# Loading cached keys by groups of 32 tokens instead of by head, in a hybrid decoder layer on one Trainium2 core

## The chip, the core and the metric

The kernel runs on one core of a Trainium2 chip. The core has five engines, each with an instruction queue of its own that is worked off in order: TensorE (PE; its weight loads are listed apart as PEld), VectorE (DVE), ScalarE (ACT), GpSimd (POOL) and SyncE (SP), which here issues transfers. A transfer is carried out by the core's 16 DMA engines, in packets. The metric is the device time of one execution in microseconds; less is better.

## The reference

One layer of a decoder serves a prompt of 512 tokens and a group of 8 sample sequences with 4 new tokens each, with the same weights, all in float32. Its three sub-layers are a mixer (4 mLSTM heads and 4 differential-attention heads), a cross-attention with 4 heads of 256 into 256 memory tokens, and a gated feed-forward network with a short causal convolution. What the change touches are the keys that the sample group reads from its caches:

```python
past_k = cache_dk[l][page_table].reshape(Bs, past_len, DA_HEADS, 2, DA_QK_DIM)   # 8 x 256 x 4 x 128

def mem_attend(h, mk, mv, w_mq, w_mo):
    q = (h @ w_mq).reshape(B, T, MEM_HEADS, MEM_HEAD_DIM)
    s = jnp.einsum('bqhd,bkhd->bhqk', q, mk) * (MEM_HEAD_DIM ** -0.5)            # mk: 8 x 256 x 4 x 256
    p = jax.nn.softmax(s, axis=-1)
    o = jnp.einsum('bhqk,bkhd->bqhd', p, mv).reshape(B, T, D_MODEL)
    return o @ w_mo
```

Per sequence there are two pages of 128 past tokens, found through `page_table`, with 4 heads of 128 (512 KB), and 256 memory tokens with 4 heads of 256 (1 MB). A cache row is one token: its heads lie side by side in DRAM.

## The kernel before

The kernel is one program for the Tile framework: it is written in a sensible order, and the framework's scheduler orders each engine's instructions and puts in the waits. Weights stream from DRAM through six staging tiles (`stage()`, named `wst`, 128 partitions x 1024), are split into a high and a low part by ScalarE (line 146) and VectorE (line 147) and then used by TensorE; transfers wait until such a tile is free. Large products are `gemmA` (lines 411 to 413) and `gemmB` (lines 472 and 485). All large loads go through SyncE's queue.

**Token keys** (`dk_load`, lines 1215 to 1221). For each of the 8 sequences a staging tile takes the keys of two pages. TensorE wants the key dimension on the partitions. So head h's 32 tokens out of a group are put on partitions 32h to 32h + 31, four groups of 32 tokens side by side, and `dk_turn` (line 1224) transposes 32 x 32 blocks in place on VectorE. Each transfer serves one head of one page: 32 partitions, on each of them 4 rows of 512 B from tokens that lie 32 apart; 8 transfers a sequence, 64 in all, 64 KB each. The page's number is read from a table, so a register operation stands ahead of each transfer. The scores (`dk_scores`, line 1251) go to `sc`, are summed into `pS` (line 1264) and are followed by the softmax. The prompt's differential attention (`da_soft`, `da_turn`, `da_av`: lines 1275 to 1305) is interleaved with this, a step at a time, and shares VectorE with it. Four of the six staging tiles hold mLSTM states until these are written out (line 1010), so six of the eight sequences are loaded after that, and then the values (line 1090, tile `vt`) and `w_out`.

**Memory keys** (`mk_load`, lines 1507 to 1513). For each sequence two tiles of 128 tokens, from the staging tiles (`wst`), the weight slots (`kvt`) or a spare tile. The layout is the same: 32 partitions for each head, 4 rows of 1,024 B on each, one transfer for each head of each half: 8 transfers a sequence, 64 in all, 128 KB each. `mk_turn` (line 1517) transposes each tile, 16 times in all. `gemmB`'s second half for the queries (line 485 with `hqT`; its results are taken from PSUM by lines 1439 and 1440, on ScalarE and VectorE) runs while the first sequences load. Then come the prompt's cross-attention (`ch_soft`, `ch_turn`, `ch_out`: lines 1460 to 1493), the sample group's scores (line 1529), their sum (line 1540) and softmax, the values (`mv_load`, line 1557, 512 KB each) and their product (line 1567, into `pso`). `oS` (line 1611) takes that from PSUM, `ost` (line 1614) transposes it, and the product with `w_mo` follows. The sample group's convolution state is loaded in the same stretch (lines 1626 to 1628).

The convolution outputs (lines 1785 and 1786, tile `cvr`) are transfers of another kind, which the prediction uses: they write 8 partitions to 2 x 4 rows of 512 B in DRAM, and 64 partitions to 16 x 4 rows.

Of the kernel before, what the change touches and what calls it, by code (L numbers as in the profile page):

```python
# [15 lines left out]
P = 128  # L16
# [4 lines left out]
NS = NB * TS  # L21
ROWS = SEQ + NS
H = 4
# [54 lines left out]
def kernel(ctx: ExitStack, tc: tile.TileContext, I, O):  # L78
# [29 lines left out]
    def T2(shape, name, dt=F32):  # L108
        return t2p.tile(list(shape), dt, name=name, tag="T2")
# [17 lines left out]
    def v2(t, b):  # L127
        return t.rearrange("p (a b) -> p a b", b=b)
# [10 lines left out]
    dma = nc.sync.dma_start  # L139
# [69 lines left out]
    def stage():  # L209
        return stg.tile([P, 1024], F32, name="wst", tag="st")  # L210
# [319 lines left out]
    for b in range(2):  # L530
        kept.append(norm_turn(xms[b], P, "g_mem_src", memT, b * P))
        if b == 0:

            t = turned[0].ins
            fill = mmp("fill")
            for _ in range(NFILL):
                with burst(t):
                    t = mm(fill, lhsT=warm[:, 0:P], rhs=warm, start=True, stop=True).ins
# [132 lines left out]
    for c0, c1 in HALF:  # L671
        n = c1 - c0
# [4 lines left out]
        t = T2([64, n], "gt")  # L677
# [253 lines left out]
    for g in range(2):  # L931
        for h in range(0, H, 2):
            t = stage().rearrange("p (j b e) -> p j b e", j=2, b=4)
# [38 lines left out]
    t = None  # L972
    for h in range(H):
        with burst(t):
            t = mm(pg[NS * h:NS * h + NS, P:2 * P + 1], lhsT=sm_t[:, h, :], rhs=vNs[:, h, :], start=True, stop=True).ins
    for h in range(H):
        with burst(t):
            t = mm(pg[NS * h:NS * h + NS, 4:12], lhsT=qT[:, h, SEQ:], rhs=nT[:, h, :], start=True, stop=True).ins
    for b in range(NB):
        for h in range(H):  # L980
            with burst(t):
                t = mm(pi[NS * h:NS * h + NS, 0:P], lhsT=qzm[:, 256 * h + b * NS:256 * h + (b + 1) * NS],
                       rhs=csts[b // 4, h][:, b % 4, :], start=(b == 0), stop=(b == NB - 1)).ins
# [101 lines left out]
    def page(name, b, g):  # L1085
        v = nc.sync.value_load(ptab[0:1, 2 * b + g:2 * b + g + 1], min_val=0, max_val=I[name].shape[1] - 1)
        return I[name][0, bass.ds(v, 1)]
# [120 lines left out]
    for b in range(4):  # L1208
        c = slice(b * P, b * P + P)
# [3 lines left out]
    kst, pts, aTs, outs, rcs = {}, {}, {}, {}, {}  # L1213

    def dk_load(b):
        st = kst[b] = stage()
        for g in range(2):
            src = page("cache_dk", b, g)
            for h in range(H):
                dma(out=v2(st[NS * h:NS * h + NS, 512 * g:512 * g + 512], P),  # L1220
                    in_=src[:, :, h].rearrange("n (k t) d -> t (n k) d", t=NS))

    def dk_turn(b):
        nc.vector.transpose(out=kst[b], in_=kst[b])
# [93 lines left out]
    for t, _ in enumerate(pipe(NB, dk_load, dk_turn, dk_scores)):  # L1318
        if t == 3:
            F.add(out_gate())  # L1320
        F.run(2.5)
        next(prompt)
        F.run(2.5)
# [86 lines left out]
    for q in range(2):  # L1410
        st = v2(stage(), 256)
        dma(out=st, in_=mk_d[:, 4 * q:4 * q + 4])
        split(mkT[0][:, 4 * q:4 * q + 4], mkT[1][:, 4 * q:4 * q + 4], st)
    for c in range(2):
        st = stage()
# [79 lines left out]
    kst, vts = {}, {}  # L1495
# [4 lines left out]
    def two(i):  # L1500

        if i < 3:
            return [stage(), stage()]
        t = wp.tile([P, 2, DM], F32, name="kvt", tag="W") if i < 7 else S([P, 2, DM], F32, "kvt")
        return [t[:, 0], t[:, 1]]

    def mk_load(b):

        kst[b] = two(home[b])
        for c in range(2):  # L1510
            for h in range(H):
                dma(out=v2(kst[b][c][NS * h:NS * h + NS], 256),
                    in_=I["cache_mem_k"][0, b, c * P:(c + 1) * P, h].rearrange("(k t) d -> t k d", t=NS))

    def mk_turn(b):
        for t in kst[b]:
# [2 lines left out]
    def mk_scores(bs):  # L1519

        t = None
        for b in bs:
            ps = mmp("ssc")[:, :256]
            for c in range(2):
                kv = kst[b][c].rearrange("p (k j t) -> p k j t", j=8, t=NS)
                for j in range(8):
                    g = NS * (j % 4)
                    with burst(t):
                        t = mm(v2(ps[g:g + NS, c * P:c * P + P], NS), lhsT=qx[:, j, b // 2 * 2:b // 2 * 2 + 2].rearrange("p n r -> p (n r)"),
                               rhs=kv[:, :, j, :], start=(j < 4), stop=(j >= 4)).ins  # L1530
            nc.scalar.copy(out=sc[:, b], in_=ps)
        return t
# [40 lines left out]
    for k in range(4):  # L1573
        mk_load(SEQS[k])
    for i, _ in enumerate(gemmB(hqT, [ev_q(m) for m in range(4, 8)])):
        if i % 4 == 1:
            mk_turn(SEQS[i // 4])
        if i % 4 == 3:
            mk_load(SEQS[4 + i // 4])
# [11 lines left out]
    t = mk_scores(SEQS[4:])  # L1591
# [205 lines left out]
    for gi, js in enumerate(groups):  # L1797
# [8 lines left out]
        def one(b, ps, i, s, cs=slice(0, 512)):  # L1806
            t = act[i // 2][:, i % 2]
            st, en = i == 0, i == nk - 1
            if b == 4:
                return sample_mm(ps, [acs[i], acs[i + 1]], s[1], i == 0, i == nk - 2)  # L1810
            s = s[0]
            c0 = b * P
            mm(ps, lhsT=t[:, 0, c0:c0 + P], rhs=s[:, 0, i % 2, cs], start=st, stop=False)  # L1813
            mm(ps, lhsT=t[:, 0, c0:c0 + P], rhs=s[:, 1, i % 2, cs], start=False, stop=False)  # L1814
            return mm(ps, lhsT=t[:, 1, c0:c0 + P], rhs=s[:, 0, i % 2, cs], start=False, stop=en)  # L1815
# [29 lines left out]
        if not last:  # L1845
            behind = []
            for n0 in (0, 512):
# [4 lines left out]
                for i in range(nk):  # L1852
# [3 lines left out]
                    for b in range(4):  # L1856
                        t = one(b, ps[b], i, s)
# [14 lines left out]
        def chunk(b, n0):  # L1872
            while len(wd) < (nk // 2 if n0 == 0 else nk):
                wd.append(W.get())
            w = 256 if (b, n0) == (TORD[-1], 512) else 512
            for o in range(0, 512, w):
                ps = mmp()[:, :w]
                for i in range(0, nk, 2 if b == 4 else 1):
                    t = one(b, ps, i, wd[(n0 and nk // 2) + i // 2], slice(o, o + w))
                add_y(b, ps, n0 + o, w)  # L1880
            return t
# [39 lines left out]
        t = chunk(TORD[1], 0)  # L1921

        for n0 in (0, 512):
            with burst(t.ins):
                t = chunk(TORD[0], n0)
# [78 lines left out]
```

## Time and profile before

| | before |
|---|---|
| median of 3 runs | 962.47 us (960.28 to 964.78) |
| profiled execution | 962.62 us, its span 960.9 us |
| granted TensorE clock, mean | 0.983 of full speed |
| TensorE busy, matmul / weight load | 918.8 us (96%) / 798.7 us (83%) |
| VectorE / ScalarE / GpSimd busy | 602.7 / 373.1 / 206.7 us |
| read from DRAM / written | 112.31 MB / 16.93 MB |
| token keys issued | 213.8 to 273.5 us after the span's start |
| memory keys issued | 401.6 to 447.8 us |

The span runs from the first to the last instruction. An engine's busy share is a mean over stages with different limits; what a stage is limited by is read from its waits. In a list of waits a row names who waited, for whom, and then the total, the number and the longest, in microseconds. In an engine's order of time a row has start, duration, engine, line, operation, out<-in and a count of merged instructions, and in brackets the idle time before it and what ended it. `SPq` rows are SyncE's transfers: the duration is that of the issuing instruction, not of the data. A DMA view of a window has the packets in it, their sizes and the share of the 16 engines' time that they took.

### The profile page before, as it was taken

To read this page: it belongs to the slowest core of one execution; us is meant where nothing else is said; L and a number is where in the kernel's file an instruction comes from. 1 tells how busy PE (TensorE), PEld (TensorE's weight loads), DVE (VectorE), ACT (ScalarE), POOL (GpSimd) and SP (SyncE) were. 2 spreads that over 40 slices of the span, in tenths; PEclk is the share of its full clock that TensorE was granted. 3 is DMA by queue.
4 is the path that set the end of the run, shared out by engine and by line. 5 is a ranking of instruction groups with operands and counts; after the bars stand their busy time and mean duration, and the time that the engine had idled before them with its cause. 6 is when DMAs were issued, how large, how long until landed. Compare 5 with 4: busy or idle time off the path is not lost. (4 is left out here: it accounts for less than half of the span.)

```text
span 960.9 us, 17244 instructions
## 1 busy us (share of the span) xinstructions
PE 918.8 (96%) x6584; PEld 798.7 (83%) x6584; DVE 602.7 (63%) x1108; ACT 373.1 (39%) x715; POOL 206.7 (22%) x422
## 2 busy tenths in 40 slices
PE   8999999999679999979979999999999999999995
PEld 5899787889546778979857899989988997999974
DVE  5846145654787338666644678727758676676767
ACT  5745233344366447613523534232212222122222
POOL 6610000107422216301000363101101110110114
PEclk9999999999899999989979999999999999999998
DMA  8950023353573339988752842053052412612023
GB/s 283 313 173 2 8 81 135 88 166 92 165 244 125 132 115 305 291 179 225 292 203 88 231 154 89 4 161 103 4 141 71 131 26 68 174 48 88 23 92 115
DMA packets 134498, 130.37 MB, mean 136 GB/s; under 512 B 10103, under 2 KB 104152, under 8 KB 134416
## 3 DMA queue, kind: packets, MB, share of 16 engines
q1 hardware_dynamic: 128232, 125.70, 43.2%
q10 hardware_dynamic: 6184, 3.57, 1.2%
q8 instruction: 52, 0.85, 0.4%
q14 instruction: 30, 0.25, 0.1%
HBM read 112.31 MB, written 16.93 MB: 135 GB/s over the span
## 5 line engine op out<-in xcount | busy, mean ns | idle before, releaser
L485 PE MATMUL mm<-fT,wslot 128*128 128x256 f32 x1872 | 236.0, 288 | 0.0
L485 PEld LDWEIGHTS mm<-fT,wslot 128*128 128x128 f32 x1872 | 234.4, 188 | 1.8 <-issue 0.8
L146 ACT CAST wslot<-wst 128x1024 fp32r<-128x1024 f32 x125 | 130.7, 1049 | 261.3 <-issue 80.4
L147 DVE TENSOR_TENSOR wslot<-wst,wslot 128x1024 fp32r<-128x1024 f32 x125 | 154.4, 1239 | 86.4 <-ACT wslot L146 85.9
L1814 PE MATMUL mm<-wslot,act 128*128 128x512 f32 (+1 forms) x180 | 70.2, 391 | 0.0
L1815 PE MATMUL mm<-wslot,act 128*128 128x512 f32 (+1 forms) x180 | 70.0, 392 | 0.0
L1813 PE MATMUL mm<-wslot,act 128*128 128x512 f32 (+1 forms) x180 | 69.3, 387 | 0.0
L1719 POOL COPY cvo<-u 128x2 f32<-128x2 f32 x43 | 10.4, 242 | 204.5 <-DVE u L1717 194.5
L411 PE MATMUL mm<-wslot,hT 128*128 128x512 f32 x128 | 51.3, 402 | 0.0
L413 PE MATMUL mm<-wslot,hT 128*128 128x512 f32 x128 | 51.0, 400 | 0.0
L412 PE MATMUL mm<-wslot,hT 128*128 128x512 f32 x128 | 50.8, 397 | 0.0
L485 PE MATMUL mm<-hT,wslot 128*128 128x256 f32 (+1 forms) x384 | 50.8, 289 | 0.0
L1714 DVE TENSOR_TENSOR u<-mm,rsb 128x256 f32<-128x256 f32 x43 | 18.1, 424 | 50.6 <-PE mm L485 50.3
L485 PEld LDWEIGHTS mm<-hT,wslot 128*128 128x128 f32 x384 | 49.1, 188 | 0.5 <-issue 0.2
L1813 PEld LDWEIGHTS mm<-wslot,act 128*128 128x128 f32 x180 | 34.3, 191 | 8.0 <-issue 0.8
L1815 PEld LDWEIGHTS mm<-wslot,act 128*128 128x128 f32 x180 | 33.8, 188 | 7.2 <-issue 0.4
L1814 PEld LDWEIGHTS mm<-wslot,act 128*128 128x128 f32 x180 | 33.8, 188 | 7.2
L1731 ACT ACTIVATE c<-c 128x560 f32<-128x560 f32 x21 | 14.1, 672 | 56.6 <-DVE c L1725 56.6
L1725 DVE SCALAR_TENSOR_TENSOR c<-u,cvT,c 128x560 f32<-128x560 f32 x43 | 34.3, 797 | 0.9
L1724 DVE SCALAR_TENSOR_TENSOR c<-u,cvT,c 128x560 f32<-128x560 f32 x43 | 34.1, 793 | 0.2
L485 PE MATMUL mm<-hqT,wslot 128*128 128x256 f32 x192 | 27.0, 305 | 5.0 <-ACT qs L1442 5.0
L485 PEld LDWEIGHTS mm<-hqT,wslot 128*128 128x128 f32 x192 | 26.4, 204 | 5.4 <-ACT qs L1442 5.4
(482 smaller groups left out, 1818.2 us busy)
## 6 DMA issues: line engine op xcount, KB each, us to landing
wst<-in_w_up_dram SPq DMA_DIRECT2D x42, 512.0 KB
wst<-in_w_in_dram SPq DMA_DIRECT2D x28, 512.0 KB
wst<-in_w_down_dram SPq DMA_DIRECT2D x20, 512.0 KB
kvt<-in_cache_mem_k_dram SPq DMA_DIRECT2D x40, 128.0 KB
kvt<-in_cache_mem_v_dram SPq DMA_DIRECT2D x10, 512.0 KB
wst<-in_w_mk_dram SPq DMA_DIRECT2D x8, 512.0 KB
xb<-in_x_prompt_dram SPq DMA_DIRECT2D x8, 512.0 KB
wst<-in_cache_dk_dram SPq DMA_DIRECT2D x64, 64.0 KB
```

Source lines behind the costliest of these rows:

```text
L146: nc.scalar.copy(out=hi, in_=src)
L147: (eng or nc.vector).tensor_tensor(out=lo, in0=src, in1=f32(hi), op=SUB)
L411: mm(ps[b], lhsT=xt.hi(k, c0, c0 + n), rhs=s[:, 0, kk, :], start=(k == 0), stop=False)
L412: mm(ps[b], lhsT=xt.hi(k, c0, c0 + n), rhs=s[:, 1, kk, :], start=False, stop=False)
L413: return mm(ps[b], lhsT=xt.lo(k, c0, c0 + n), rhs=s[:, 0, kk, :], start=False, stop=(k == nk - 1))
L485: mm(ps[i], lhsT=s[:, l, k, :], rhs=x(k, c0, c1), start=(k == 0 and j == 0), stop=(k == 7 and j == 2))
L1714: VTT(out=u[:, 2:258], in0=ps, in1=rsb[:, 0:256], op=MUL)
L1724: STT(out=c, in0=u[:, 1:EXT - 1], scalar=w[1], in1=c, op0=MUL, op1=ADD)
L1725: STT(out=c, in0=u[:, 0:EXT - 2], scalar=w[0], in1=c, op0=MUL, op1=ADD)
L1813: mm(ps, lhsT=t[:, 0, c0:c0 + P], rhs=s[:, 0, i % 2, cs], start=st, stop=False)
L1814: mm(ps, lhsT=t[:, 0, c0:c0 + P], rhs=s[:, 1, i % 2, cs], start=False, stop=False)
L1815: return mm(ps, lhsT=t[:, 1, c0:c0 + P], rhs=s[:, 0, i % 2, cs], start=False, stop=en)
```

## The change

The 8 transfers of a sequence's keys are cut in another way. Before, one transfer took one head and all four groups of 32 tokens. Now one takes one group of 32 tokens and all four heads. It writes 128 partitions with one row each, instead of 32 partitions with four rows each. In DRAM it reads 4 heads of 32 tokens, instead of 32 tokens of 4 groups. Each byte lands where it landed before; the number of transfers, their sizes and the rows' lengths (512 and 1,024 B) are the same, and so are the transposes and all that follows.

```diff
         for g in range(2):
             src = page("cache_dk", b, g)
-            for h in range(H):
-                dma(out=v2(st[NS * h:NS * h + NS, 512 * g:512 * g + 512], P),
-                    in_=src[:, :, h].rearrange("n (k t) d -> t (n k) d", t=NS))
+            for k in range(4):
+                dma(out=st[:, 512 * g + P * k:512 * g + P * k + P], in_=src[:, NS * k:NS * k + NS].rearrange("n t h d -> (n h) t d"))
...
         kst[b] = two(home[b])
         for c in range(2):
-            for h in range(H):
-                dma(out=v2(kst[b][c][NS * h:NS * h + NS], 256),
-                    in_=I["cache_mem_k"][0, b, c * P:(c + 1) * P, h].rearrange("(k t) d -> t k d", t=NS))
+            for k in range(4):
+                dma(out=kst[b][c][:, 256 * k:256 * k + 256], in_=I["cache_mem_k"][0, b, c * P + NS * k:c * P + NS * k + NS].rearrange("t h d -> h t d"))
```

The file is two lines shorter, so line numbers behind each place are one and two lower in the changed kernel. The scheduler makes a slightly different order of it. SyncE's queue at the memory keys, from the first of them to the first values (`wst` and `kvt` are the keys' and values' tiles, `cr` the convolution state), before:

```order
L1512 DMA kvt<-in_cache_mem_k_dram 32x4x256 x3
L1512 DMA wst<-in_cache_mem_k_dram 32x4x256 x8
L1512 DMA kvt<-in_cache_mem_k_dram 32x4x256 x5
L1512 DMA wst<-in_cache_mem_k_dram 32x4x256 x16
L1512 DMA kvt<-in_cache_mem_k_dram 32x4x256 x16
L1626 DMA cr<-in_state_conv_dram 16x896
L1512 DMA kvt<-in_cache_mem_k_dram 32x4x256 x8
L1627 DMA cr<-in_w_dw_dram 3x896
L1628 DMA cr<-in_b_dw_dram 1x896
L1626 DMA cr<-in_state_conv_dram 16x896
L1512 DMA kvt<-in_cache_mem_k_dram 32x4x256 x8
L1557 DMA wst<-in_cache_mem_v_dram 128x1024 x2
```

and with the change:

```order
L1511 DMA kvt<-in_cache_mem_k_dram 128x1x256 x2
L1511 DMA wst<-in_cache_mem_k_dram 128x1x256 x8
L1511 DMA kvt<-in_cache_mem_k_dram 128x1x256 x4
L1511 DMA wst<-in_cache_mem_k_dram 128x1x256 x4
L1511 DMA kvt<-in_cache_mem_k_dram 128x1x256 x2
L1511 DMA wst<-in_cache_mem_k_dram 128x1x256 x12
L1511 DMA kvt<-in_cache_mem_k_dram 128x1x256 x16
L1624 DMA cr<-in_state_conv_dram 16x896
L1511 DMA kvt<-in_cache_mem_k_dram 128x1x256 x16
L1555 DMA wst<-in_cache_mem_v_dram 128x1024 x6
```

The keys stand together as before, with the written shape 128 x 1 x 256 instead of 32 x 4 x 256; three small convolution loads have moved behind the keys, and the third tile's loads stand between two other tiles' loads.

VectorE's order at the third token sequence's transpose (the STREAM_TRANSPOSE; `mltm` belongs to the mLSTM's output gate, `rc` and `pda` to the prompt's softmax, `nm` is its maximum), before:

```order
L1045 TENSOR_TENSOR mltm<-mlt,soT 128x512
L1281 RECIPROCAL rc<-su 128x2
L1224 STREAM_TRANSPOSE wst<-wst 128x1024
L1045 TENSOR_TENSOR mltm<-mlt,soT 128x512
L1283 SCALAR_TENSOR_TENSOR pda<-pda,rc 128x128
L1045 TENSOR_TENSOR mltm<-mlt,soT 128x512
L1282 TENSOR_SCALAR rc<-rc,su,nlam 128x1
L1045 TENSOR_TENSOR mltm<-mlt,soT 128x128
```

and with the change:

```order
L1045 TENSOR_TENSOR mltm<-mlt,soT 128x512 x2
L1281 TENSOR_SCALAR rc<-rc,su,nlam 128x1 x2
L1045 TENSOR_TENSOR mltm<-mlt,soT 128x512
L1045 TENSOR_TENSOR mltm<-mlt,soT 128x128
L1282 SCALAR_TENSOR_TENSOR pda<-pda,rc 128x128
L1223 STREAM_TRANSPOSE wst<-wst 128x1024
L1282 SCALAR_TENSOR_TENSOR pda<-pda,rc 128x128
```

The gate's products and one `pda` step of the prompt have moved ahead of this transpose.

ScalarE's order where the sample group's cross-attention is taken from PSUM (`wslot<-wst` are casts of `w_mo`), as a piece of the difference:

```order
-L146 CAST wslot<-wst 128x1024 x3
-L1611 COPY oS<-pso 128x256
-L146 CAST wslot<-wst 128x1024
...
+L146 CAST wslot<-wst 128x1024 x2
+L1609 COPY oS<-pso 128x256
+L146 CAST wslot<-wst 128x1024
```

`oS` has moved ahead of the third cast of `w_mo`.

## The prediction

> **What bounds the kernel now.** I read the page first, then the list of waits on TensorE, then VectorE's and SyncE's instructions in order of time at the two places that the change touches, last the DMA views of short windows. The page and the waits:
>
> ```profile
> PE 918.8 (96%) x6584; PEld 798.7 (83%) x6584; DVE 602.7 (63%) x1108; ACT 373.1 (39%) x715; POOL 206.7 (22%) x422
> PE   8999999999679999979979999999999999999995
> ...
> PE ost L1614 <- ACT oS L1611: 6.1, 1, 6.1
> PE tpa L1291 <- DVE pda L1283: 5.2, 2, 5.0
> PE mm L485 <- ACT qs L1442: 5.0, 2, 3.8
> ```
>
> TensorE is the bound, 96% busy, and has few holes; but the three longest lie at the token keys (the 6 and the 7 of the second row, 240 to 288 us, in slices of 24 us) and at and behind the memory keys (the next two 7s, from 408 and from 480 us). Behind the second and the third stands VectorE, which transposes each key tile when it has landed and takes everything else behind it in order:
>
> ```profile
> 254.22 1.25 DVE L1224 STREAM_TRANSPOSE wst<-wst 128x1024 f32<-128x1024 f32 x1 [3.08 <-DMA wst<-in_cache_dk_dram]
> 258.73 1.25 DVE L1224 STREAM_TRANSPOSE wst<-wst 128x1024 f32<-128x1024 f32 x1 [0.20 <-DMA wst<-in_cache_dk_dram]
> ...
> 275.93 1.23 DVE L1224 STREAM_TRANSPOSE wst<-wst 128x1024 f32<-128x1024 f32 x1
> ...
> 413.24 1.25 DVE L1517 STREAM_TRANSPOSE wst<-wst 128x1024 f32<-128x1024 f32 x1 [7.40 <-DMA wst<-in_cache_mem_k_dram]
> ...
> 433.08 1.25 DVE L1517 STREAM_TRANSPOSE kvt<-kvt 128x1024 f32<-128x1024 f32 x1 [1.23 <-DMA kvt<-in_cache_mem_k_dram]
> 435.40 1.25 DVE L1517 STREAM_TRANSPOSE kvt<-kvt 128x1024 f32<-128x1024 f32 x1 [1.08 <-DMA kvt<-in_cache_mem_k_dram]
> ...
> 452.02 1.23 DVE L1517 STREAM_TRANSPOSE kvt<-kvt 128x1024 f32<-128x1024 f32 x1
> ```
>
> The bracket is VectorE's idle time and what ended it. Both key streams already set its pace: a token sequence (8 transfers) every (275.93 - 254.22) / 5 = 4.34 us, half a memory sequence (4 transfers) every 2.3 to 2.4 us. So there is almost no slack ahead of either stream. What paces them is seen on SyncE and in the DMA views (427 to 436 us for the memory keys, 256 to 266 for the token keys, 285 to 289 for w_out):
>
> ```profile
> 213.77 0.43 SPq L1220 DMA_DIRECT2D wst<-in_cache_dk_dram  x1
> ...
> 224.95 0.32 SPq L1220 DMA_DIRECT2D wst<-in_cache_dk_dram  x1
> ...
> 253.67 20.19 SPq L1220 DMA_DIRECT2D wst<-in_cache_dk_dram  x38
> ...
> 401.62 3.65 SPq L1512 DMA_DIRECT2D kvt<-in_cache_mem_k_dram  x3
> ...
> 427.26 8.97 SPq L1512 DMA_DIRECT2D kvt<-in_cache_mem_k_dram  x16
> ```
>
> ```profile
> DMA packets 2190, 2.00 MB, mean 222 GB/s; under 512 B 241, under 2 KB 2190, under 8 KB 2190
> ```
>
> ```profile
> DMA packets 2748, 1.28 MB, mean 128 GB/s; under 512 B 303, under 2 KB 2746, under 8 KB 2746
> q1 hardware_dynamic: 2746, 1.25, 45.2%
> wst<-in_cache_dk_dram SPq DMA_DIRECT2D x19, 64.0 KB
> ```
>
> ```profile
> DMA packets 814, 1.51 MB, mean 378 GB/s; under 512 B 76, under 2 KB 76, under 8 KB 814
> ```
>
> Token keys: 20.19 / 38 = 0.53 us a transfer with the DMA engines 45% busy, so SyncE's issuing paces them. Memory keys: about 0.6 us a transfer at 222 GB/s, where w_out reaches 378 GB/s with all 128 partitions, so the transfer itself paces them. The smallest packets close a transfer, one for each DMA engine that took part: 19 token transfers and 303 of them, 16 each.
>
> **The change, part by part.** The bytes and the 64 + 64 transfers stay. Each now writes 128 rows of one head-and-token block, but reads DRAM as 4 heads by 32 tokens; before, both sides had 32 rows. The trace has a pair of that kind, the convolution outputs: L1785 writes 8 partitions to 2 x 4 rows (4 KB), L1786 64 partitions to 16 x 4 rows (32 KB). Their issue, beside today's keys (min/median/max ns), and their packets, in a window that holds the packets of the 4 KB one alone and in one with both:
>
> ```profile
> L1220 SPq DMA_DIRECT2D wst<-in_cache_dk_dram x64: 316/317/1236, 213.8 to 273.5; - x64
> L1512 SPq DMA_DIRECT2D kvt<-in_cache_mem_k_dram x40: 311/430/2693, 401.6 to 447.8; - x40
> L1785 SPq DMA_DIRECT2D out_dram<-cvr x10: 644/657/772, 605.6 to 917.6; - x10
> L1786 SPq DMA_DIRECT2D out_dram<-cvr x10: 591/602/647, 606.5 to 918.3; - x10
> ```
>
> ```profile
> DMA packets 10, 0.00 MB, mean 2 GB/s; under 512 B 2, under 2 KB 10, under 8 KB 10
> ```
>
> ```profile
> DMA packets 90, 0.04 MB, mean 15 GB/s; under 512 B 18, under 2 KB 90, under 8 KB 90
> ```
>
> 8 rows on one side and 2 on the other ran on 2 engines; 64 and 16 ran on 16 (18 - 2). Not the side in SBUF but what both sides share sets the number. For 128 and 4 that makes 4 engines instead of 16. This is the step on which the forecast rests.
>
> Issue: 0.60 to 0.66 us instead of 0.32 (token) and 0.43 (memory). With what SyncE does besides for a token key, 0.53 - 0.32 = 0.21 us, a token transfer takes 0.81 to 0.87 us to issue.
>
> Row time on one engine: 512 B takes 0.452 x 16 x 10 us / 2746 packets = 26 ns, or 29 ns if the closing ones weigh little; 2,048 B takes 2048 x 16 / 378 = 87 ns (w_out). A 1,024 B row lies between, 29 + (87 - 29) / 3 = 48 ns. The other end is what 1,024 B rows take today: 1024 x 16 / 222 = 74 ns. I take 48 ns: four engines at that speed ask for 85 GB/s, far below the 222 that the same rows reach into only 32 partitions now.
>
> Whether successive transfers use the same four engines no row shows. If each went to other engines, they would cost nothing and issue would set the pace; if always to the same four, a transfer takes 32 rows in turn. I take the second, as nothing in a transfer tells it from the next.
>
> [...]
>
> *Token keys.* 32 x 29 ns = 0.93 us a transfer (issue, 0.87 us at most, is just under it), 7.4 us a sequence instead of 4.34: for the six sequences from 254 us on, 6 x 3.1 = 18 us. The first two: 16 x 0.93 = 14.9 us against 224.95 - 213.77 = 11.2 us of issuing, 4 us. VectorE has about 1 us of lead at the end (275.93 came without a wait). Together **+21 us**. Behind the late transposes stand the prompt's softmax steps in VectorE's order, and TensorE for them; the order moves one of these ahead of the third sequence's transpose, which shortens the 5.0 us wait but not the stream behind it.
>
> *Memory keys.* 32 x 48 ns = 1.54 us a transfer, 64 of them 98 us. They start some 2 us behind the first issue at 401.62, so the last transpose stands at about 503 us instead of 452.0: 50 us. What TensorE can do meanwhile, and what shrinks behind it:
>
> ```profile
> 454.99 3.70 PE L1529 MATMUL ssc<-kvt,qx 128*32 128x128 f32 x128
> ...
> 492.47 0.69 PE L1614 MATMUL ost<-cpk,oS 128*128 128x128 f32 x2 [6.11 <-ACT oS L1611]
> ```
>
> ```profile
> 481.80 3.06 SPq L231 DMA_DIRECT2D wst<-in_w_mo_dram  x6
> ```
>
> Of the last score matmuls three quarters (2.8 us), and about 1.7 us of prompt work ahead of them, no longer come after the last key: -4.5 us. The 6.1 us hole comes from w_mo, whose cast stands ahead of oS on ScalarE and whose issue at 481.80 stood behind value and convolution loads; by then these will be through, and one cast fewer stands ahead: about -4.5 us. The values, 8.4 MB, follow the keys as now. Together **+41 us**. Were there cover for this stream, it would have to be work on VectorE ahead of the transposes, and there is none.
>
> Sum, against the profiled execution's own 962.6 us (span 960.9 and 1.7 around it; the median of the runs, 962.47, is the same): 962.6 + 21 + 41 = **1025 us**.
>
> **Rivals.**
> *Four engines that hinder each other.* Two heads written in step could meet at the same place of SBUF, as today's 16 engines over 32 partitions seem to (74 ns). Then memory keys take 64 x 32 x 74 ns = 152 us, 54 us more, and token rows 37 ns, 9.5 us a sequence, some 17 us more: 1095 us. Against it: the four need not run in step, so half of that, 1060, is likelier than all. [...]
> *All 16 engines, slow issue.* If the 128 partitions decide after all, or the groups of four rotate, only issue is left: token keys 0.84 us a transfer, 6 x 8 x 0.84 = 40 us against 26, and 2 us for the first two, less 1, +15; memory keys 0.63 + 0.05 us against 0.6, some +4. 982 us. Against it speaks the 4 KB transfer's 2.
> *Faster.* If in addition issue stays at 0.32 and 0.43 us, memory keys would go at SyncE's 0.48 us a transfer, VectorE's waits for them would end, and with them TensorE's 5.0 us and the clock lost behind it:
>
> ```profile
> 415.00:425.00 10.00, 5.02 (x36) 4.61 (x35) 8.82 (x10) 1.61 (x4) 0.91 (x4) 0.87 0.67 154
> 425.00:435.00 10.00, 10.00 (x66) 10.00 (x66) 5.80 (x7) 1.60 (x6) 0.92 (x4) 0.79 1.10 225
> ```
>
> (the clock is the last column but two): 3 us, so 962.6 - 8 = 955 us. This decides once a memory transfer takes under 0.6 us. For it: 378 against 222 GB/s. Against it: the four issue rows and the 2.
>
> **How the numbers follow.** Four engines unhindered 0.65 (its own range 1005 to 1050, from the two ends of the savings and of the row time a little above 48 ns); hindered 0.18; 16 engines with slow issue 0.12; faster or no change 0.05. The range 975 to 1085 leaves out the faster case, some of the second rival and the upper half of the first. A change under 0.5% is what a measurement of this kernel can't tell from none: faster 0.04, same 0.02, slower 0.94.
>
> **What would show it.** The changed keys' issue rows at 0.6 to 0.66 us; in a window of memory keys alone 4 closing packets a transfer (one in 33 packets), not 16, and some 85 GB/s; VectorE's memory transposes 6.2 us apart, the token ones 7.4; TensorE's holes between 255 and 300 and between 410 and 505 us; the gaps behind unchanged. 16 closing packets a transfer, or memory transposes closer than 3 us, would prove the forecast wrong; transposes 9 us apart would speak for hindrance.

## The result, and the profile after

The changed kernel takes 1029.2 us (median of 4 runs, 1028.7 to 1030.5), the kernel before in the same comparison 962.8 us: a ratio of 1.069, with a 95% interval of 1.067 to 1.072. The forecast was 1025 us. The traced execution has a span of 1027.3 us (before: 960.9) and a mean granted clock of 0.954 (0.983), so 66.4 us are to be found between the two spans.

TensorE is busy 17 us longer and 5 points less of the span. On the page, its two lines, the second in 40 slices of 25.7 us:

```profile
PE 936.0 (91%) x6584; PEld 811.3 (79%) x6584; DVE 606.8 (59%) x1108; ACT 373.4 (36%) x715; POOL 207.8 (20%) x422
...
PE   8999999998479999937487999999999999999995
```

The holes are where they were before, but deeper: 8, 4, 7 from 231 to 308 us at the token keys, and 3, 7, 4, 8, 7 from 437 to 565 us at the memory keys. Nothing new opens behind them.

VectorE's transposes of the token keys (first and second row, one sequence apart, then the last one), and of the memory keys (from the middle of the stream two that follow each other, then the last one):

```profile
260.81 1.25 DVE L1223 STREAM_TRANSPOSE wst<-wst 128x1024 f32<-128x1024 f32 x1 [5.82 <-DMA wst<-in_cache_dk_dram]
267.43 1.25 DVE L1223 STREAM_TRANSPOSE wst<-wst 128x1024 f32<-128x1024 f32 x1 [4.51 <-DMA wst<-in_cache_dk_dram]
...
295.28 1.25 DVE L1223 STREAM_TRANSPOSE wst<-wst 128x1024 f32<-128x1024 f32 x1 [2.55 <-DMA vt<-in_cache_dv_dram]
...
479.74 1.25 DVE L1515 STREAM_TRANSPOSE kvt<-kvt 128x1024 f32<-128x1024 f32 x1 [4.55 <-DMA kvt<-in_cache_mem_k_dram]
485.40 1.25 DVE L1515 STREAM_TRANSPOSE kvt<-kvt 128x1024 f32<-128x1024 f32 x1 [3.77 <-DMA kvt<-in_cache_mem_k_dram]
...
521.60 1.25 DVE L1515 STREAM_TRANSPOSE kvt<-kvt 128x1024 f32<-128x1024 f32 x1 [4.92 <-DMA kvt<-in_cache_mem_k_dram]
```

A token sequence now comes every 6.6 us at first, and in the mean of the five intervals every (295.28 - 260.81) / 5 = 6.9 us instead of 4.34; half a memory sequence comes every 5.7 us instead of 2.3 to 2.4. Ahead of most memory transposes VectorE stands for 3 to 5 us and waits for the transfer, ahead of the token ones for 1 to 6 us. What the transfers do in that time is in two DMA views, of the memory keys from 468 to 488 us, and of the token keys from 258 to 288 us (the first line is the busy share of the 16 engines in tenths, in 40 slices):

```profile
DMA packets 1848, 1.85 MB, mean 93 GB/s; under 512 B 56, under 2 KB 1847, under 8 KB 1847
q1 hardware_dynamic: 1847, 1.83, 27.2%
```

```profile
DMA  2222233333333333333232333333333233333233
DMA packets 4809, 2.42 MB, mean 81 GB/s; under 512 B 146, under 2 KB 4806, under 8 KB 4806
q1 hardware_dynamic: 4806, 2.39, 30.0%
```

Of the memory keys' packets 56 are closing ones, one in 33: 4 for each transfer of 128 rows, not 16. The packets fill 27.2% of 16 engines, that is 4.4 engines' time, at 93 GB/s instead of 222, so the 4 closing packets are read as 4 engines. A row of 1,024 B takes 0.272 x 16 x 20 us / 1847 = 47 ns (the packets' times overlap a little: before, from 427 to 436 us, they add up to 112.6% of 16 engines' time; so a transfer takes 1.42 us, the spacing below, and not 32 x 47 ns = 1.50). The token keys show the same: 146 closing packets for the window's 36 to 37 transfers, 4 each, and a share that stays at 2 to 3 tenths without a gap.

How the late memory keys reach TensorE is seen in its list of waits, and in ScalarE's order of time:

```profile
PE mm L485 <- ACT qs L1441: 16.0, 2, 8.0
```

```profile
448.03 0.20 ACT L1441 ACTIVATE qs<-mm 128x32 f32<-128x32 f32 x1 [15.57 <-DVE ql L1439]
```

TensorE's products for the queries wait until ScalarE's `qs` has taken the last ones, `qs` waits for VectorE's `ql`, and `ql` (at 447.58 us) stands in VectorE's order behind the first three key transposes (436.76, 442.44 and 445.31 us). Before, this wait of TensorE was 5.0 us.

SyncE's issues of both kinds, by line (min/median/max ns):

```profile
L1220 SPq DMA_DIRECT2D wst<-in_cache_dk_dram x64: 532/565/1282, 213.1 to 289.5; - x64
L1511 SPq DMA_DIRECT2D kvt<-in_cache_mem_k_dram x40: 562/1342/1782, 423.6 to 511.6; - x40
```

and two pieces of SyncE's order of time:

```profile
256.14 33.97 SPq L1220 DMA_DIRECT2D wst<-in_cache_dk_dram  x41
...
466.67 22.79 SPq L1511 DMA_DIRECT2D kvt<-in_cache_mem_k_dram  x16
```

A token transfer takes 33.97 / 41 = 0.83 us, a memory one 22.79 / 16 = 1.42 us. The second row was not forecast: 1.34 us for one issue, where 0.60 to 0.66 was expected. With the rest of its loop this is just the spacing of the stream, so from the trace alone the issue could be the cause as well as the four engines. The experiments have to decide that.

To see where the 66.4 us come in, one needs points that all later work follows. In TensorE's order of time these are the first `w_out` product behind the token keys, the sums of the memory scores and the transposed output. Before:

```profile
348.92 0.51 PE L412 MATMUL mm<-wslot,mixT 128*128 128x512 f32 x1 [0.30 <-DVE wslot L147]
...
460.62 1.07 PE L1540 MATMUL pS<-sc,cpk 128*32 128x256 f32 x16
```

and in the changed kernel:

```profile
370.48 0.50 PE L412 MATMUL mm<-wslot,mixT 128*128 128x512 f32 x1 [0.30 <-DVE wslot L147]
...
527.20 1.07 PE L1538 MATMUL pS<-sc,cpk 128*32 128x256 f32 x16
...
558.24 0.69 PE L1612 MATMUL ost<-cpk,oS 128*128 128x128 f32 x2 [5.38 <-DMA wst<-in_w_mo_dram]
```

| stretch | forecast | measured |
|---|---|---|
| token keys, to the first `w_out` product | +21 | 370.48 - 348.92 = +21.6 |
| from there to the last memory transpose | +50 | 521.60 - 452.02 - 21.6 = +48.0 |
| from there to the sums | -4.5 | (527.20 - 521.60) - (460.62 - 452.02) = -3.0 |
| from there to the transposed output | -4.5 | (558.24 - 527.20) - (492.47 - 460.62) = -0.8 |
| from there to the end | 0 | (1027.3 - 558.24) - (960.9 - 492.47) = +0.6 |
| sum | +62 | +66.4 |

### The profile page after: what moved, and what is told of

It reads as the page before. It is cut to its first block, busy times and chain, and to the rows that moved or that the text cites. A ratio compares the mean times of both kernels' runs of the same rounds, so it can differ in the third digit from the quotient of the medians.

```text
span 1027.3 us, 17241 instructions
## 1 busy us (share of the span) xinstructions
PE 936.0 (91%) x6584; PEld 811.3 (79%) x6584; DVE 606.8 (59%) x1108; ACT 373.4 (36%) x715; POOL 207.8 (20%) x422
## 5 line engine op out<-in xcount | busy, mean ns | idle before, releaser
L485 PE MATMUL mm<-hqT,wslot 128*128 128x256 f32 x192 | 31.6, 335 | 23.3 <-ACT qs L1441 16.0
L485 PEld LDWEIGHTS mm<-hqT,wslot 128*128 128x128 f32 x192 | 30.6, 233 | 24.2 <-ACT qs L1441 16.5
```

What stands on the lines that cost most here:

```text
L485: mm(ps[i], lhsT=s[:, l, k, :], rhs=x(k, c0, c1), start=(k == 0 and j == 0), stop=(k == 7 and j == 2))
```

## The experiments

### Each half of the change alone

Token keys alone are the first hunk of the diff, memory keys alone the second.

> Only the token keys are cut by tokens; the memory keys stay cut by head. Four engines (theory): the token stream alone costs what it cost in the changed kernel, where everything behind it stands 21.5 us later (first hole-free point behind it: 348.92 us before, 370.48 after), so 962.8 + 21.5 = 984 us; transposes of a token sequence 6.6 us apart, memory transposes 2.3 to 2.4 us apart as before. Rival, the two parts share a cost (a queue that is behind from the tokens on makes the memory keys late too): 990 us or more.

> Only the memory keys are cut by tokens; the token keys stay cut by head. Four engines: the rest of the difference, 1029.2 - 962.8 - 21.5 = 45 us, so 1008 us; memory transposes 5.7 us apart; the wait of the transposed output for its copy about as long as in the changed kernel (5.4 us), not the 1.6 us that was forecast. Rival, parts not additive: more than 3 us from 1008.

Measured: token keys alone 985.25 us, ratio 1.023 (1.021 to 1.025) to 963.5 us, so +21.8 us; memory keys alone 1009.2 us, 1.048 (1.045 to 1.051), +45.8 us. Together 67.6 us, the whole change 66.4: the two parts add up, within what the runs can tell, and share no cost. With the token keys alone their first sequences behind the mLSTM states come 6.6 us apart and the memory transposes in the middle of their stream about 2.5; with the memory keys alone their transposes come 5.7 us apart. The wait for the transposed output, in the lists of waits of the one and of the other:

```profile
PE ost L1613 <- ACT oS L1610: 6.3, 1, 6.3
```

```profile
PE ost L1613 <- ACT oS L1610: 5.2, 1, 5.2
```

The late memory keys took 0.9 us off the 6.1, not the 4.5 of the forecast.

### The long issue without the four engines

The changed transfers take longer to issue than those of before (0.57 us a token transfer instead of 0.32). With a switch of the language, `dge_precook`, transfers in the shapes of before take a long issue too (0.58 us a token transfer in the run below); that it is the same long way is concluded from the like times alone:

```diff
+            nc.dge_precook = False
             for h in range(H):
                 dma(out=v2(st[NS * h:NS * h + NS, 512 * g:512 * g + 512], P), ...
+            nc.dge_precook = True
```

and in the same way around the memory keys' loop.

> Shapes as before (32 rows on both sides, 16 engines), but the 128 key transfers are issued by the longer way, as the changed ones are. Four engines: issue rows rise to about 0.6 us, 16 closing packets a transfer stay, a token transfer costs 0.6 + 0.21 = 0.81 us instead of 0.53, a memory one 0.65 instead of 0.6; 962.8 + 15 + 4 = 982 us, so most of the 66 us isn't the issue. Rival, the issue itself paces the changed streams (its rows there take 0.57 and 1.33 us, which with 0.25 and 0.1 us besides is just the spacing of 0.83 and 1.43 us): issue rows of 1.3 us at the memory keys here too, and close to 1029 us.

Measured: 978.4 us, 1.017 (1.015 to 1.020). The traced execution was the fastest of five (its span 970.9 us). Its issues by line, then the DMA view of its token keys from 262 to 272 us, then the third and the last transpose of a token sequence:

```profile
L1221 SPq DMA_DIRECT2D wst<-in_cache_dk_dram x64: 580/581/986, 213.2 to 283.8; - x64
...
L1515 SPq DMA_DIRECT2D kvt<-in_cache_mem_k_dram x40: 577/599/2737, 412.7 to 461.6; - x40
```

```profile
DMA  0620440440370350261005302603502602600701
DMA packets 1744, 0.81 MB, mean 81 GB/s; under 512 B 192, under 2 KB 1743, under 8 KB 1743
```

```profile
254.48 1.25 DVE L1226 STREAM_TRANSPOSE wst<-wst 128x1024 f32<-128x1024 f32 x1 [2.44 <-DMA wst<-in_cache_dk_dram]
...
286.74 1.25 DVE L1226 STREAM_TRANSPOSE wst<-wst 128x1024 f32<-128x1024 f32 x1 [1.86 <-DMA wst<-in_cache_dk_dram]
```

The 192 closing packets are one in 9, 16 for a transfer of 128 rows. The long way costs 0.58 to 0.60 us an issue for both kinds, and 15 us in all. So the 1.34 us of the changed memory keys are no price of the issue: something holds it back. At the token keys the two causes nearly meet. With the long issue alone a sequence comes every (286.74 - 254.48) / 5 = 6.45 us, at the same 81 GB/s as with four engines; only here the DMA engines run in bursts with gaps (0 to 7 tenths), so the issue is the limit, and in the changed kernel they run without a gap, so the four engines are. The first `w_out` product behind the token keys stands at 361.31 us here, 12.4 us later than before: of the 21.6 us that the token keys cost in the changed kernel, the long issue alone would have cost more than half.

### Two issuers for the same four engines

```diff
-                dma(out=kst[b][c][:, 256 * k:256 * k + 256], ...
+                (dma, nc.scalar.dma_start)[k % 2](out=kst[b][c][:, 256 * k:256 * k + 256], ...
```

> The changed kernel, with every second memory-key transfer issued by ScalarE on its own queue, the others by SyncE. Always the same four engines (theory): two issuers don't help, the memory keys still take 94 us (1.47 us a transfer), some 90 GB/s; 1029 us, or up to 10 us more, as ScalarE's own work stands behind its issues. Rivals, the issue paces the stream (1.33 us rows) or each queue has four engines of its own: about 47 us, some 180 GB/s, 1029 - 45 = 984 us.

Measured: 1029.0 us, ratio to before 1.069 (1.066 to 1.072), the same as the changed kernel. The DMA view of the memory keys from 450 to 465 us (q1 is SyncE's queue, q10 ScalarE's), and SyncE's issues by line:

```profile
DMA packets 1370, 1.37 MB, mean 92 GB/s; under 512 B 42, under 2 KB 1368, under 8 KB 1368
q1 hardware_dynamic: 684, 0.68, 13.5%
q10 hardware_dynamic: 684, 0.68, 13.5%
```

```profile
L1511 SPq DMA_DIRECT2D kvt<-in_cache_mem_k_dram x20: 528/529/3054, 420.4 to 506.6; - x20
```

Both queues carry the same number of packets, and together they reach the 92 GB/s of one. The issue row falls from 1.34 to 0.53 us and nothing becomes faster. That settles both open points: the issue doesn't pace the memory keys, and successive transfers, even from another queue, go to the same four engines; with four engines of its own for each queue the rate could have doubled. The trace doesn't name engines: that they are always the same is read from the 92 GB/s and from the packets of both queues, which together fill 27.0% of 16 engines, 4.3 engines' time, as those of the one queue filled 27.2%.

### Two engines instead of four

```diff
-            for h in range(H):
-                dma(out=v2(kst[b][c][NS * h:NS * h + NS], 256), ...
+            for k in range(4):
+                for h in (0, 2):
+                    dma(out=kst[b][c][NS * h:NS * h + 64, 256 * k:256 * k + 256], in_=I["cache_mem_k"][0, b, c * P + NS * k:c * P + NS * k + NS, h:h + 2].rearrange("t h d -> h t d"))
```

> Token keys as before. Memory keys by two heads of 32 tokens: 128 transfers of 64 KB, 64 partitions on one side, 2 x 32 rows on the other. What both sides share sets the number of engines (theory): 2 engines, 2 closing packets a transfer, 46 GB/s, the stream takes 128 x 32 x 46 ns = 188 us, the last transpose at about 405 + 188 + 3 = 596 us instead of 452; 962.8 + 144 - 4 = 1103 us. Rival, four engines whenever the sides differ: 94 us, 1009 us. Rival, all that matters is the number of transfers by a 1.33 us issue: also some 180 us, but with 4 or 16 closing packets a transfer.

Measured: 1085.4 us, 1.127 (1.123 to 1.131). The DMA view from 450 to 470 us, and in VectorE's order of time two transposes of the middle and the last one:

```profile
DMA packets 923, 0.93 MB, mean 47 GB/s; under 512 B 28, under 2 KB 922, under 8 KB 922
```

```profile
468.61 1.25 DVE L1517 STREAM_TRANSPOSE wst<-wst 128x1024 f32<-128x1024 f32 x1 [9.56 <-DMA wst<-in_cache_mem_k_dram]
480.05 1.25 DVE L1517 STREAM_TRANSPOSE wst<-wst 128x1024 f32<-128x1024 f32 x1 [9.56 <-DMA wst<-in_cache_mem_k_dram]
...
593.65 1.25 DVE L1517 STREAM_TRANSPOSE kvt<-kvt 128x1024 f32<-128x1024 f32 x1 [7.40 <-DMA wst<-in_cache_mem_v_dram]
```

Again one closing packet in 33, now for transfers of 64 rows, so 2 a transfer: 2 engines, as the packets fill 13.6% of 16, 2.2 engines' time. The rate halves to 47 GB/s and the transposes lie 11.4 us apart, twice 5.7. The last transpose stands at 593.65 us (forecast 596). The time was forecast 18 us too high: of the 142 us by which the last key is late, only 122 come through. Two things in the trace go that way: TensorE does some of the prompt's next steps ahead of the last key (from 583.4 to 589.7 us), and the wait for the transposed output is gone from the list of waits. What each of them gave is not shown. Four and two engines both fit the number that both sides share, and nothing else that was proposed.

### 128 partitions with all engines

```diff
-... src[:, NS * k:NS * k + NS].rearrange("n t h d -> (n h) t d")
+... src[:, NS * k:NS * k + NS].rearrange("n t h d -> (n t h) d")
-... I["cache_mem_k"][0, b, ...].rearrange("t h d -> h t d")
+... I["cache_mem_k"][0, b, ...].rearrange("t h d -> (t h) d")
```

> Transfers of the changed kernel with the 128 rows taken in DRAM's own order, so that both sides count 128. The rows land on other partitions: the sample group's two sets of scores are made from mixed-up keys, all else is done as before. Four engines: now all 16 take part (16 closing packets a transfer) and the issue is short; token keys as before (0.53 us a transfer, issue-paced), memory keys at SyncE's 0.48 us, no waits of VectorE for them: 955 us. Rival, writing 128 partitions is itself what is slow: 1029 us. Rival, the 74 ns rows of before do not come from 32 partitions: memory transfers stay at 0.6 us, 962 us.

Measured: 955.8 us, 0.993 (0.991 to 0.996): faster than before. The memory keys' issues by line and a piece of SyncE's order of time, and the DMA view of their stream from 425 to 435 us:

```profile
L1511 SPq DMA_DIRECT2D kvt<-in_cache_mem_k_dram x40: 328/430/1532, 405.4 to 444.2; - x40
...
425.95 7.49 SPq L1511 DMA_DIRECT2D kvt<-in_cache_mem_k_dram  x16
```

```profile
DMA packets 2891, 2.64 MB, mean 264 GB/s; under 512 B 328, under 2 KB 2885, under 8 KB 2891
```

So writing 128 partitions one row each is not what is slow. With 128 rows on both sides the issue is short (0.43 us in the median, as before), about one packet in 9 is a closing one (16 a transfer), and the stream reaches 264 GB/s, above the 222 of before. These 264 are no limit of the transfers: their packets fill only 87% of the 16 engines' time, and SyncE issues one every 7.49 / 16 = 0.47 us, which for 128 KB is 280 GB/s at most. The same transfers cost 1029.2 - 955.8 = 73 us more when DRAM is read as 4 x 32. This run also reads DRAM in one piece, but reading it in pieces is not what is slow: the kernel before reads 1,024 B out of every 4,096 and reaches 222 GB/s. What this run gains can't be had by this kernel as it is, since the rows stand on partitions where the transposes and the scores don't look for them.

### What limits the memory keys of before

Two runs give the heads of the kernel before to two queues, by the order of issue heads 0 and 1 are on their way together in one of them, then 2 and 3 (these lie 32 partitions apart), and in the other 0 and 2, then 1 and 3 (64 apart). In DRAM the two heads that are on their way together lie 1,024 B apart in the first run and 2,048 B in the second. Nothing else differs between the two; the second run's edit:

```diff
-            for h in range(H):
-                (dma, nc.scalar.dma_start)[h % 2](out=v2(kst[b][c][NS * h:NS * h + NS], 256), ...
+            for h in (0, 2, 1, 3):
+                (dma, nc.scalar.dma_start)[h // 2](out=v2(kst[b][c][NS * h:NS * h + NS], 256), ...
```

> The kernel before, with every second head of the memory keys issued by ScalarE. If the 222 GB/s of before are what 16 engines can put into 32 partitions at a time (the flat rows reached 264 GB/s), two heads at once make 260 to 330 GB/s, the last transpose comes 4 to 8 us earlier, 955 to 959 us. Rival, ScalarE's issues of 0.4 us and their waits for free tiles hold up its casts and the queries' evictions, on which TensorE waits already (3.8 us): the same or slower, 963 to 970 us.

> As in the run with two queues by head, but SyncE issues heads 0 and 1 and ScalarE heads 2 and 3, in the order 0, 2, 1, 3, so that the two heads on their way together lie 64 partitions apart, not 32. Nothing else differs, on any engine. If partitions 32 apart share their way into SBUF (theory; then heads 0 and 1 together get no more than one alone, as the 211 GB/s of that run suggest), 0 and 2 together get more: 260 GB/s or above in the memory keys, and 2 to 6 us off the 966 us. Rival, the limit lies on DRAM's side or in the engines (rows of 1 KB, 4 KB apart): 211 GB/s and 966 us again.

Measured: 966.4 us, 1.003 (1.002 to 1.005), and 965.3 us, 1.001 (1.000 to 1.002). Both streams from 431 to 440 us, where the DMA engines are full (the packets add up to 112% and 111% of their time), the first with partitions 32 apart, the second 64 apart:

```profile
DMA packets 2126, 1.98 MB, mean 220 GB/s; under 512 B 252, under 2 KB 2109, under 8 KB 2125
```

```profile
DMA packets 2556, 2.33 MB, mean 259 GB/s; under 512 B 283, under 2 KB 2556, under 8 KB 2556
```

Heads 0 and 1 together get the 220 GB/s that one head gets alone; heads 0 and 2 together get 259 (248 against 218 in the window from 430 to 435 us, 238 against 219 from 435 to 440). This speaks for 32 partitions as what limits the memory keys of before, and a head 32 partitions further doesn't widen the way; that the distance in DRAM plays no part is not shown. The time didn't follow: the forecast of 955 to 959 us for the first run and that of 2 to 6 us off for the second were both wrong. The last memory transposes of the two runs, 32 and 64 apart:

```profile
454.96 1.25 DVE L1517 STREAM_TRANSPOSE kvt<-kvt 128x1024 f32<-128x1024 f32 x1 [0.62 <-DMA kvt<-in_cache_mem_k_dram]
```

```profile
453.94 1.25 DVE L1517 STREAM_TRANSPOSE kvt<-kvt 128x1024 f32<-128x1024 f32 x1 [0.42 <-DMA kvt<-in_cache_mem_k_dram]
```

Both come 2 to 3 us later than the 452.02 of before, and only 1 us from each other. Part of this is the start: the third memory transpose comes at 421.75 us in the second run and at 418.86 in the first, so the second stream loses 2.9 us ahead and wins back 3.9. And neither stream holds its rate: in the last quarter of a view from 430 to 445 us the means are 156 and 205 GB/s. What holds them up was not followed further.

### The wait that did not shrink

The transposed output waits because ScalarE casts `w_mo` first, and `w_mo`'s loads stand behind the convolution loads on SyncE. Here these 24 small loads are issued by ScalarE, once in the kernel before and once in the changed one:

```diff
-        dma(out=t[p0:p0 + 16, o:o + n], in_=conv0[:, c0:c0 + n])
+        nc.scalar.dma_start(out=t[p0:p0 + 16, o:o + n], in_=conv0[:, c0:c0 + n])
```

and so the two lines behind it.

> The kernel before, with the 24 small loads of the convolution state issued by ScalarE instead of SyncE. Forecast and failed: the 6.1 us wait of the transposed output would shrink where w_mo's loads come sooner. If these stand too late in SyncE's queue because of the convolution loads ahead of them (issued at 481.80 us, when their staging tiles were last read at 476), they are issued about 5 us earlier, the wait goes to 1 or 2 us and the kernel to about 958 us. Rival, the wait depends on something else (a staging tile, the casts): it stays near 6 us and 963 us.

> The changed kernel, with the 24 small loads of the convolution state issued by ScalarE. If these loads, which moved along with the keys, are why the wait of the transposed output stayed at 5.4 us where it was forecast to shrink to 1.6 (theory), it goes to 0 to 2 us here too, and the time from 1029 to about 1020 us, as in the kernel before (9 us). Rival, in the changed kernel the values, which come behind the keys, hold up w_mo's loads: the wait stays at 4 us or more, 1025 to 1029 us.

Measured: 954.0 us, 0.991 (0.988 to 0.994), in the kernel before; 1018.0 us, 1.057 (1.055 to 1.059) to before, in the changed kernel, 11 us below the 1029.2. In neither does the list of waits have the transposed output any more. SyncE's `w_mo` rows, first in the kernel before with this edit:

```profile
474.06 7.58 SPq L231 DMA_DIRECT2D wst<-in_w_mo_dram  x6
```

then in the changed kernel, with the last convolution load ahead of them:

```profile
547.34 0.25 SPq L1626 DMA_DIRECT2D cr<-in_b_dw_dram  x1
...
548.99 4.26 SPq L231 DMA_DIRECT2D wst<-in_w_mo_dram  x6
```

and in the changed kernel with this edit, where the last memory transpose comes 3 us later than without it:

```profile
543.15 5.51 SPq L231 DMA_DIRECT2D wst<-in_w_mo_dram  x6
```

```profile
524.81 1.25 DVE L1515 STREAM_TRANSPOSE kvt<-kvt 128x1024 f32<-128x1024 f32 x1 [3.15 <-DMA wst<-in_cache_mem_v_dram]
```

In the changed kernel `w_mo` was issued 67 us later than before (548.99 against 481.80), as late as the keys themselves: values and convolution loads stand in order behind the key transfers and had moved along with them. Without the convolution loads it goes 6 us earlier, although the keys come 3 us later. The transposed output itself then comes no earlier (559.27 against 558.24), but the products with `w_mo` do: they start at 558.82 us instead of 562.98. The gain of 9 us in the kernel before is more than the wait of 6.1: the clock comes on top. In windows of that place, in the kernel before without and with the edit (the clock is the last column but two):

```profile
475.00:500.00 25.00, 18.46 (x157) 13.37 (x150) 12.65 (x31) 8.92 (x20) 0.00 (x0) 0.81 0.63 229
```

```profile
475.00:500.00 25.00, 23.34 (x193) 16.54 (x185) 12.77 (x32) 8.75 (x20) 0.00 (x0) 1.00 0.71 255
```

Behind the hole TensorE runs at a lower clock for some time: the products with `w_mo` follow each other every 0.43 us up to 500.8 us and every 0.23 from there on. With the edit, where there is no hole, the clock stays at 1.00 and they follow every 0.23 us from the first.

### Two issuers for the token keys

Last, the first statement of the prediction's reading is tried on the kernel with the convolution loads moved: the second page of each sequence's token keys goes to ScalarE's queue.

```diff
+            eng = (nc.sync, nc.scalar)[g]
-            src = page("cache_dk", b, g)
+            src = page("cache_dk", b, g, eng)
             for h in range(H):
-                dma(out=v2(st[NS * h:NS * h + NS, 512 * g:512 * g + 512], P),
+                eng.dma_start(out=v2(st[NS * h:NS * h + NS, 512 * g:512 * g + 512], P),
```

> The kernel before with the convolution loads on ScalarE (954 us alone), and besides, the second page of each sequence's token keys is issued by ScalarE too (32 of the 64 transfers, with their page numbers read there). If SyncE's issue paces the token keys of before (0.53 us a transfer with the DMA engines 45% busy: the first step of the reading), a sequence comes in 2.2 to 3 us instead of 4.34, and the transposes go at VectorE's own pace: 2 to 8 us off, 946 to 952 us. Rival, ScalarE's own steps of the prompt's softmax stand behind its issues, which wait for free tiles: TensorE waits for them, 954 us or slower. Rival, the reading is wrong and the transfers set the pace: no closer transposes, 954 us.

Measured: 953.0 us, 0.990 (0.986 to 0.994), against 954.0 without it: no difference that can be told. The third and fourth transpose, and the last two:

```profile
254.29 1.25 DVE L1225 STREAM_TRANSPOSE wst<-wst 128x1024 f32<-128x1024 f32 x1 [0.50 <-DMA wst<-in_cache_dk_dram]
...
259.29 1.24 DVE L1225 STREAM_TRANSPOSE wst<-wst 128x1024 f32<-128x1024 f32 x1
...
270.60 1.24 DVE L1225 STREAM_TRANSPOSE wst<-wst 128x1024 f32<-128x1024 f32 x1
...
273.23 1.23 DVE L1225 STREAM_TRANSPOSE wst<-wst 128x1024 f32<-128x1024 f32 x1
```

Behind the first of these none waits for a transfer any more, so the issue did pace the token keys. But they come (273.23 - 254.29) / 5 = 3.8 us apart, 5.0 in the first interval and 2.6 in the last, where 2.2 to 3 were forecast: VectorE has the prompt's softmax beside them, is busy for 21.8 of the 25 us from 250 on, and is the next limit. 2 to 8 us were forecast and did not come.

## Why the prediction was right, step by step

**The number of engines: right.** Four closing packets a transfer, 93 GB/s, and two closing packets and 47 GB/s for the two-headed transfers. The step had been read off two output transfers of the kernel before, one of them with 2 closing packets; it held for transfers 32 times as large.

**Always the same four: right.** No row of before showed it; the run with two queues does (92 GB/s with two, 93 with one).

**Not hindered: right.** 47 ns for a row of 1,024 B against the 48 taken, where the rival had 74. Had the rival held, memory transposes would lie 9 us apart; they lie 5.7. The 48 ns had come from a straight line between two other lengths, 29 ns for 512 B and 87 ns for 2,048 B. No row of before lay on that line, and the 29 was too high, as the token keys show; with 26 ns it gives 46.

**Token keys, +21: the sum right, its parts not.** A row was taken at 29 ns, 0.93 us a transfer and 7.4 us a sequence; measured are 0.83 us a transfer and 6.6 to 6.9 us a sequence, nearer to the 26 ns that the window of before gave with the closing packets counted. The five intervals from the third to the last sequence grew by (295.28 - 260.81) - (275.93 - 254.22) = 12.8 us, where 3.1 us each, 15.3 us, were forecast. The third sequence itself came 260.81 - 254.22 = 6.6 us late, where 4 us were forecast for the first two and 3.1 for its own. So the stream was forecast 3 us too long. Against that stand 1 us of VectorE's lead that was taken off, and 2 us that came behind the last transpose and were not forecast (21.6 - 6.6 - 12.8). The errors cancelled; that the sum is so close is luck.

**Issue: right at the token keys, not at the memory keys.** 0.57 us is a little below the 0.60 to 0.66 taken, and as forecast just under what the engines need. That the memory keys' issue rows would stand at 1.34 us was missed: they show how long the issue was held back, not what it costs (0.53 us when two queues share the work, 0.60 us when 16 engines take the rows).

**Memory keys, +50: nearly right.** +48.0; the stream ran at 1.42 us a transfer with one issue after another, not at 1.54, and the last transpose stands at 500.0 us once the 21.6 us of the tokens are taken off, where 503 was forecast.

**The first saving, -4.5: -3.0.** The part of it from score matmuls and prompt work that no longer come after the last key.

**The second saving, -4.5: wrong.** This is the step that failed: "by then these will be through, and one cast fewer stands ahead". The value and convolution loads were not through, because they stand behind the keys in SyncE's order and moved along; the saving up to the transposed output was 0.8 us. The runs with the convolution loads on ScalarE show what was in their way: 11 us in the changed kernel, 9 us in the kernel before. Only where the keys took twice as long again, with two engines, did the wait vanish by itself.

**The rivals' prices.** All 16 engines with the long issue: 982 forecast, 978.4 measured. All 16 with the short issue: 955 forecast, 955.8 measured. Neither was what the change did, but each was worked out from the right rows.

**What would show it.** The 4 closing packets a transfer came as named, and so did the holes at the two streams and the unchanged gaps behind them. The rate was a little higher (93 GB/s, not 85) and the transposes closer (token keys 6.6 to 6.9 us, not 7.4; memory keys 5.7, not 6.2). The memory keys' issue rows did not come as named: 1.34 us, not 0.60 to 0.66.

## What to carry to other kernels

Before a transfer is cut in another way, count its outermost dimension on both sides: with 128 and 128 a transfer had 16 closing packets here and reached 264 GB/s, with 128 and 4 it had 4 and 93 GB/s, with 64 and 2 it had 2 and 47 GB/s, all with rows of 1,024 B, so more partitions on one side did not make up for few on the other. Of the other transfers, those with 32 and 32 had 16, with 64 and 16 also 16, with 8 and 2 they had 2; more pairs were not tried. An issue row that grows in the same step as the stream can be the victim and not the cause; a second issuer tells the two apart (here the row fell from 1.34 to 0.53 us, and the rate stayed at 92 GB/s). And when a stream becomes later, everything behind it in the same queue does too (`w_mo` was issued 67 us later), so a gap further on doesn't fill by itself; the 24 small loads that were taken out of that queue gave the one version that does all of the layer's work and is faster than both kernels (954.0 us, 0.9% below before; 953.0 with the token keys on two queues).

## What was not expected of the hardware

Transfers into partitions 32 apart shared 220 GB/s, 64 apart they reached 259, with the same lengths of rows, engines and queues. How far rows of 1,024 B over all 128 partitions can go is open: their 264 GB/s were paced by SyncE's issuing, and what lies between them and the 378 GB/s of `w_out`, whose packets are twice as long, was not tried. And a hole in TensorE's work cost more than its length: with the 6.1 us wait gone, 9 us were gained, as the clock stayed at 1.00 from 475 to 500 us, where its mean had been 0.81.
